# Where the weights' parts lie in SBUF against the tokens' parts, and three 256-column products per block in a gated short-convolution layer

## The chip, the cores and the metric

The kernel runs on one core of one Trainium2 chip. Times are device microseconds (us). The kernel before takes 954.23 us, the median of three runs (953.26 to 955.2). Engines: PE is TensorE (PEld its weight loads), DVE is VectorE, ACT is ScalarE, SP issues the DMAs.

## The reference, cut to what matters

One layer on 256 tokens of width 2048, with branches of width E = 4096, all in float32:

```python
h = rmsnorm(x, norm_g)                                  # (256, 2048)
shift, scale, gate = split(silu(c) @ ada_w + ada_b, 3)  # ada_w: 2048 x 6144
h = h * (1 + scale) + shift
b, cg, v, g = split(h @ w_in, 4)                        # w_in: 2048 x 16384
u = causal_depthwise_conv(cg * v, conv_w)               # three taps
y = b * u * silu(g)
x = x + gate * (y @ w_out)                              # w_out: 4096 x 2048
return rmsnorm(x, final_g)
```

## The kernel before, in words

**Split products.** Matmuls run in float32r. To keep float32's accuracy every operand is split into a rounded part and the rest: a weight tile `raw` becomes `hi` (ACT, L191) and `lo` (DVE, L192); the tokens become `hh` and `hl`, the first and second 256 columns of `hT[:, k, :]` (L261, L262); y becomes `yh` and `yl` (L206, L207). Each product of two matrices is then hi·hh + hi·hl + lo·hh, summed in PSUM. TensorE holds a 128x128 stationary operand and streams a moving operand past it. In the two input stages the weights' parts are stationary and the tokens' parts move; in the output stage y's parts are stationary and the weights' parts move.

**Stages.** (1) Up to about 60 us the tokens are normed and transposed, and the first sums of `ada_w` are made. (2) Up to about 410 us, the first 16 of 32 column tiles of each quarter of `w_in` (`part`, L264 to L300): four column tiles at a time, in pieces of `k` (the 16 blocks of the contraction) as `shift` and `scale` come ready, with an order that `plan()` sets. Each block (k, column tile) takes three matmuls of 256 columns: L286 hi·hh, L291 hi·hl, L292 lo·hh. Two column tiles share a PSUM bank. The sums go to `acc` (L298, L300); when a group of channels is whole, `mixed` makes y of it. DVE forms the sums of `ada_w` here as well (L238), and from about 300 us those of its gate third (`gate_piece`, L359). (3) Up to about 763 us, the two-tile stage: the other 16 column tiles, two at a time (L365 to L405), over the four quarters. Each block takes one matmul of 512 columns (L382, hi against hh and hl side by side, which fills a bank: hi·hh in its first half, hi·hl in its second) and one of 256 (L385, lo·hh into the first half). There are 8 pairs of tiles x 4 quarters x 2 tiles x 16 k = 1024 blocks. At the end of a quarter ACT copies the second half of each of the two banks to `z` (L391) and DVE adds the first (L392); the quarter's own operation follows from `z` (L396, L401, L402, L404). (4) The output stage: 4 column groups x 32 tiles x 2 token halves x 3 = 768 matmuls of 512 columns, L427 hi·yh, L428 lo·yh, L429 hi·yl. Then the gate, the second norm and the stores.

**Order and buffers.** Each engine runs its own stream in order; a scheduler with a cost model of its own sets it when the program is built. There are three buffers each for `raw`, `hi` and `lo`, all of 8192 bytes per partition, and six PSUM banks for sums.

**Places in SBUF.** Pools on the left grow upwards, pools on the right downwards from the top. In the built program `hi` and `lo` (left) start at 64 modulo 256 bytes, `hT` and the slots that hold y (right) at 224 modulo 256. All pieces inside these tiles step by multiples of 512 bytes, so that the remainders hold for every operand.

Of the kernel before, what the change touches and what calls it, by code (L numbers as in the profile page):

```python
# [8 lines left out]
F32 = mybir.dt.float32  # L9
F32R = mybir.dt.float32r  # L10
AF = mybir.ActivationFunctionType
ALU = mybir.AluOpType

P = 128
D = 2048
E = 4096
T = 256
KT = D // P
# [70 lines left out]
def short_conv_layer(ctx: ExitStack, tc: tile.TileContext, x, c, norm_g, ada_w, ada_b, w_in, conv_w, w_out, final_g, out):  # L89
    nc = tc.nc  # L90
    PSUM = bass.MemoryType.PSUM

    const = ctx.enter_context(tc.tile_pool(name="const", bufs=1))
    adap = ctx.enter_context(tc.tile_pool(name="adap", bufs=2))
    wpool = ctx.enter_context(tc.tile_pool(name="wpool", bufs=2))
    psum = ctx.enter_context(tc.tile_pool(name="psum", bufs=6, space=PSUM))
    hpool = ctx.enter_context(tc.tile_pool(name="hpool", bufs=1, side="right"))
    slots = ctx.enter_context(tc.tile_pool(name="slots", bufs=NSLOT, side="right"))

    def slot(shape, name, dtype=F32):  # L100
# [5 lines left out]
    after = mybir.DependencyInfo(mybir.DependencyClass.NoSync, mybir.DependencyReason.DATA)  # L106
# [59 lines left out]
    hT = hpool.tile([P, KT, 2 * T], F32R, tag="big", name="hT")  # L166
    hh_ = hT[:, :, 0:T]
# [40 lines left out]


    acc = {}  # L210
    gjunk = const.tile([P, P], F32, tag="gjunk", name="gjunk")
    adas = ada_w[0].rearrange("(k p) (s f) -> p k s f", p=P, s=3)

    sums = {}
# [1 line left out]
    def ada_piece(k0, nk, piece):  # L216
        w = nk * P
        kk = ASLOT // (2 * w)
        if piece == 0:
            sums[k0] = adap.tile([P, 2, 2 * P], F32, tag="gv", name="gv")  # L220
        gv = sums[k0]

        turns = [gv[:, :, i * w : (i + 1) * w] for i in range(2 if k0 == 0 and nk == 1 else 1)]
        j = piece * kk
        if k0 == 0:
            at = wpool.tile([P, SLOT], F32, tag=("lo", "hi")[piece % 2], name="at0", bufs=3)[:, :ASLOT]
        else:
            at = adap.tile([P, ASLOT], F32, tag="at", name="at", bufs=4)
        at4 = at.rearrange("p (k s f) -> p k s f", k=kk, s=2)
        for s in range(2):  # L230
            nc.sync.dma_start(at4[:, :, s, :], adas[:, j : j + kk, s, k0 * P : k0 * P + w])  # L231
        for i in range(kk):
            c_k = silu_c[:, j + i : j + i + 1]
            g2 = turns[(j + i) % len(turns)]
            if j + i < len(turns):
                nc.vector.tensor_scalar_mul(g2, at4[:, i], c_k)
            else:
                nc.vector.scalar_tensor_tensor(out=g2, in0=at4[:, i], scalar=c_k, in1=g2, op0=ALU.mult, op1=ALU.add)  # L238
        if j + kk < KT:
            return  # L240
        if len(turns) == 2:
            nc.vector.tensor_tensor(out=turns[0], in0=turns[0], in1=turns[1], op=ALU.add)

        tp = psum.tile([P, 4, P], F32, tag="sm", name="tp_g", bufs=2)
        gs = const.tile([P, 4], F32, tag="gs", name="gs", bufs=2)
        for o in range(2 * nk):
            nc.tensor.transpose(tp[:, o, :], gv[:, o // nk, (o % nk) * P : (o % nk + 1) * P], ident)
        for o in range(2 * nk):
            nc.scalar.activation(gjunk, tp[:, o, :], AF.Copy, accum_out=gs[:, o : o + 1])
        ks = slice(k0, k0 + nk)  # L250
        nc.vector.tensor_tensor(out=scale[:, ks], in0=gs[:, nk : 2 * nk], in1=b_scale[:, ks], op=ALU.add)
        nc.vector.tensor_tensor(out=shift[:, ks], in0=gs[:, 0:nk], in1=b_shift[:, ks], op=ALU.add)
        nc.vector.scalar_tensor_tensor(
            out=scale[:, ks], in0=scale[:, ks], scalar=1.0, in1=gT[:, ks], op0=ALU.add, op1=ALU.mult
        )
        for k in range(k0, k0 + nk):
            hf = xs[k // CT][:, k % CT, :]
            nc.vector.tensor_scalar(
                out=hf, in0=hf, scalar1=scale[:, k : k + 1], scalar2=shift[:, k : k + 1], op0=ALU.mult, op1=ALU.add
            )  # L260
            nc.scalar.copy(hh_[:, k], hf)  # L261
            nc.vector.tensor_tensor(out=hl_[:, k], in0=hf, in1=hh_[:, k].bitcast(F32), op=ALU.subtract)  # L262

    def part(ch, q, k0, k1):  # L264

        col = q * E + ch * CT * P
        step = SLOT // (CT * P)
        banks = [psum.tile([P, 512], F32, tag="mm", name="mm_s") for _ in range(CT // 2)]
        for s0 in range(k0, k1, step):
            sk = min(step, k1 - s0)  # L270
            n = sk * CT * P
            raw = raw_tile("raw_s")
            nc.sync.dma_start(
                raw[:, :n].rearrange("p (k f) -> p k f", k=sk),
                w_in[0, s0 * P : (s0 + sk) * P, col : col + CT * P].rearrange("(k p) f -> p k f", p=P),
            )
            hi, lo = split(raw, n)
            for i in range(sk):
                k = s0 + i
                hh, hl = hh_[:, k], hl_[:, k]  # L280
                for m in range(CT):
                    o = slice((i * CT + m) * P, (i * CT + m + 1) * P)
                    dst = banks[m // 2][:, (m % 2) * T : (m % 2 + 1) * T]

                    opens = k == k0 and m % 2 == 0
                    first = nc.tensor.matmul(dst, hi[:, o], hh, start=opens, stop=False, skip_group_check=True)  # L286
                    if opens:
                        opener = first
                    elif k == k0:
                        tc.add_manual_dep(first.ins, opener.ins.name, after, reason="the bank's flags are cleared first")  # L290
                    nc.tensor.matmul(dst, hi[:, o], hl, start=False, stop=False, skip_group_check=True)  # L291
                    nc.tensor.matmul(dst, lo[:, o], hh, start=False, stop=k == k1 - 1, skip_group_check=True)  # L292
        if k0 == 0:
            acc[ch, q] = slot([P, CT, T], f"acc{ch}{q}")
        for b, bank in enumerate(banks):
            a = acc[ch, q][:, 2 * b : 2 * b + 2, :].rearrange("p a t -> p (a t)")
            if k0 == 0:
                nc.scalar.copy(a, bank)  # L298
            else:
                nc.vector.tensor_tensor(out=a, in0=bank, in1=a, op=ALU.add)  # L300
# [65 lines left out]
    n_piece = 0  # L366
    for ct in range(NS, NCT, 2):
        for q in QUARTERS:
            banks = [psum.tile([P, 2, T], F32, tag="mm", name="mm_b") for _ in range(2)]
            col = q * E + ct * P  # L370
            for kp in range(0, KT, KP):
                raw = raw_tile("raw")
                nc.sync.dma_start(
                    raw.rearrange("p (k f) -> p k f", k=KP),
                    w_in[0, kp * P : (kp + KP) * P, col : col + 2 * P].rearrange("(k p) f -> p k f", p=P),
                )
                hi, lo = split(raw, SLOT)
                for m in range(2):
                    for i in range(KP):
                        k = kp + i  # L380
                        o = slice((i * 2 + m) * P, (i * 2 + m + 1) * P)
                        nc.tensor.matmul(  # L382
                            banks[m].rearrange("p a t -> p (a t)"), hi[:, o], hT[:, k, :], start=k == 0, stop=False, skip_group_check=True
                        )
                        nc.tensor.matmul(banks[m][:, 0, :], lo[:, o], hh_[:, k], start=False, stop=k == KT - 1, skip_group_check=True)  # L385
                n_piece += 1
                if n_piece % 2 == 0:
                    gate_piece()
            z = zs[q // 2][:, q % 2]
            for m in range(2):  # L390
                nc.scalar.copy(z[:, m, :], banks[m][:, 1, :])  # L391
                nc.vector.tensor_tensor(out=z[:, m, :], in0=banks[m][:, 0, :], in1=z[:, m, :], op=ALU.add)  # L392
            if q == 1:
                zc = z
            elif q == 2:
                nc.vector.tensor_tensor(out=zc, in0=z, in1=zc, op=ALU.mult)  # L396
                for j in range(2):
                    conv(ct + j, z[:, j, :], zc[:, j, :])
                u = z
            elif q == 3:  # L400
                nc.scalar.activation(z, z, AF.Silu)  # L401
                nc.vector.tensor_tensor(out=u, in0=u, in1=z, op=ALU.mult)  # L402
            else:
                nc.vector.tensor_tensor(out=u, in0=z, in1=u, op=ALU.mult)  # L404
                split_y(ys[ct // 2], u)  # L405
    while gate_todo:
        gate_piece()
# [118 lines left out]
```

## Time and profile before

| | |
|---|---|
| median of three runs | 954.23 us |
| the profiled execution's own time | 952.04 us |
| its span | 950.2 us |
| mean granted clock of TensorE | 0.99 |
| PE, PEld, DVE, ACT busy in the span | 918.3, 835.4, 681.4, 419.3 us |
| DMA | 227.51 MB, mean 239 GB/s |

How to read it: a matmul's duration counts from its start until its result is written, and the next one starts while it still runs, so that durations of neighbours overlap and their sum is above the span. What a matmul costs on the path is the distance between one start and the next. A weight load runs beside the matmul before the one that it is for.

### The profile page before, as it was taken

Reading aid. Unit: us, or ns where it says so; the run is one execution under the profiler, and the core shown is the slowest. Engines: PE = TensorE matmul, PEld = TensorE weight load, DVE = VectorE, ACT = ScalarE, POOL = GpSimd, SP = SyncE. Lnnn points to the kernel's source line nnn. Section 1 sums busy time; section 2 is a strip of 40 time slices with the busy share of each in tenths; the row PEclk is TensorE's granted clock in tenths of the full one; section 3 lists DMA queues with packets and bytes.
Section 4 is the critical chain, followed back from the end, with each engine's and each line's share of the span. In section 5 each row is a group of like instructions: output and inputs, shape, how many; then the busy total and the mean of one; then the engine's idle time right before and its main releaser. Section 6 shows DMA issues by size and latency. Waiting matters only on the chain.

```text
span 950.2 us, 14332 instructions
## 1 busy us (share of the span) xinstructions
PE 918.3 (97%) x5963; PEld 835.4 (88%) x5963; DVE 681.4 (72%) x789; ACT 419.3 (44%) x470; POOL 0.7 (0%) x6
## 2 busy tenths in 40 slices
PE   2799999999999999999999999999999999999996
PEld 2699999999999999988888888888888878888885
DVE  4799998999999998997465556555555654544882
ACT  6575343443435544444443444444444433343333
POOL 0000000000000000000000000000000000000000
PEclk9799999999999999999999999999999999999998
DMA  9999997999989787886665565566555685555542
GB/s 273 299 360 368 291 335 253 323 347 319 350 278 308 243 271 240 281 288 208 193 201 181 185 199 193 178 193 201 181 178 190 206 313 177 180 199 196 178 133 88
DMA packets 172048, 227.51 MB, mean 239 GB/s; under 512 B 5792, under 2 KB 112464, under 8 KB 171600
## 3 DMA queue, kind: packets, MB, share of 16 engines
q1 hardware_dynamic: 171984, 226.61, 72.9%
q8 instruction: 46, 0.75, 0.3%
q14 instruction: 18, 0.15, 0.0%
HBM read 224.49 MB, written 2.10 MB: 238 GB/s over the span
## 4 chain that ended last, share of the span: by engine, by line
PE 91%; DMA 4%; DVE 2%; issue 1%; SPq 1%; ACT 0%; ACTq 0%; DVEq 0%
PE mm_b L382 25%; PE mm_b L385 13%; PE mm_s L292 11%; PE mm_s L286 11%; PE mm_s L291 11%; PE mm_o L428 6%; PE mm_o L427 6%; PE mm_o L429 6%; DMA at<-in_ada_w_dram 2%; DMA raw_s<-in_sc_w_in_dram 2%; DVE lo L192 1%; DMA x<-in_x_dram 1%; DVE gv L238 1%; SPq L231 0%; PE ps_gate L362 0%
## 5 line engine op out<-in xcount | busy, mean ns | idle before, releaser
L382 PE MATMUL mm_b<-hT,hi 128*128 128x512 f32 x1024 | 355.2, 392 | 0.0
L286 PE MATMUL mm_s<-hT,hi 128*128 128x256 f32 x1024 | 286.9, 284 | 7.5 <-ACT hT L261 4.9
L291 PE MATMUL mm_s<-hT,hi 128*128 128x256 f32 x1024 | 287.7, 283 | 0.0
L385 PE MATMUL mm_b<-hT,lo 128*128 128x256 f32 x1024 | 285.4, 280 | 0.0
L292 PE MATMUL mm_s<-hT,lo 128*128 128x256 f32 x1024 | 283.6, 283 | 1.7 <-DVE lo L192 1.7
L192 DVE TENSOR_TENSOR lo<-raw,hi 128x2048 fp32r<-128x2048 f32 x64 | 146.6, 2291 | 128.4 <-ACT hi L191 128.4
L382 PEld LDWEIGHTS mm_b<-hT,hi 128*128 128x128 f32 x1024 | 192.0, 188 | 42.3 <-issue 0.2
L191 ACT CAST hi<-raw_s 128x2048 fp32r<-128x2048 f32 (+3 forms) x85 | 126.5, 1488 | 177.1 <-PE mm_s L291 128.6
L286 PEld LDWEIGHTS mm_s<-hT,hi 128*128 128x128 f32 x1024 | 194.4, 191 | 8.5 <-ACT hT L261 5.1
L291 PEld LDWEIGHTS mm_s<-hT,hi 128*128 128x128 f32 x1024 | 195.5, 191 | 0.2 <-issue 0.2
L292 PEld LDWEIGHTS mm_s<-hT,lo 128*128 128x128 f32 x1024 | 192.6, 191 | 2.6 <-DVE lo L192 2.4
L385 PEld LDWEIGHTS mm_b<-hT,lo 128*128 128x128 f32 x1024 | 192.3, 188 | 0.5 <-issue 0.2
L191 ACT CAST hi<-raw 128x2048 fp32r<-128x2048 f32 x64 | 122.4, 1912 | 158.0 <-PE mm_b L382 103.1
L192 DVE TENSOR_TENSOR lo<-raw_s,hi 128x2048 fp32r<-128x2048 f32 (+3 forms) x85 | 149.5, 1759 | 19.9 <-ACT hi L191 19.5
L192 DVE TENSOR_TENSOR lo<-raw_o,hi 128x2048 fp32r<-128x2048 f32 x32 | 73.3, 2290 | 67.0 <-ACT hi L191 67.0
L191 ACT CAST hi<-raw_o 128x2048 fp32r<-128x2048 f32 x32 | 61.2, 1913 | 103.8 <-PE mm_o L429 93.6
L428 PE MATMUL mm_o<-lo,y 128*128 128x512 f32 x256 | 101.7, 399 | 0.0
L427 PE MATMUL mm_o<-hi,y 128*128 128x512 f32 x256 | 101.0, 396 | 0.0
L429 PE MATMUL mm_o<-hi,y 128*128 128x512 f32 x256 | 100.1, 392 | 0.0
L238 DVE SCALAR_TENSOR_TENSOR gv<-at,silu_c,gv 128x512 f32<-128x512 f32 (+1 forms) x149 | 92.2, 639 | 3.8 <-DMA at<-in_ada_w_dram 3.0
L427 PEld LDWEIGHTS mm_o<-hi,y 128*128 128x128 f32 x256 | 48.1, 188 | 12.6 <-issue 0.2
L429 PEld LDWEIGHTS mm_o<-hi,y 128*128 128x128 f32 x256 | 48.1, 188 | 11.6
(84 smaller groups left out, 457.8 us busy)
## 6 DMA issues: line engine op xcount, KB each, us to landing
raw<-in_sc_w_in_dram SPq DMA_DIRECT2D x64, 1024.0 KB, 5.6
raw_s<-in_sc_w_in_dram SPq DMA_DIRECT2D x46, 1024.0 KB, 7.3
at<-in_ada_w_dram SPq DMA_DIRECT2D x128, 256.0 KB, 6.7
raw_o<-in_sc_w_out_dram SPq DMA_DIRECT2D x32, 1024.0 KB, 5.1
at_g<-in_ada_w_dram SPq DMA_DIRECT2D x32, 512.0 KB, 6.9
raw_s<-in_sc_w_in_dram SPq DMA_DIRECT2D x19, 512.0 KB, 5.4
raw_s<-in_sc_w_in_dram SPq DMA_DIRECT2D x7, 768.0 KB, 7.7
raw_s<-in_sc_w_in_dram SPq DMA_DIRECT2D x13, 256.0 KB, 4.4
```

Source lines behind the costliest of these rows:

```text
L191: nc.scalar.copy(hi[:, :n], raw[:, :n])
L192: nc.vector.tensor_tensor(out=lo[:, :n], in0=raw[:, :n], in1=hi[:, :n].bitcast(F32), op=ALU.subtract)
L238: nc.vector.scalar_tensor_tensor(out=g2, in0=at4[:, i], scalar=c_k, in1=g2, op0=ALU.mult, op1=ALU.add)
L286: first = nc.tensor.matmul(dst, hi[:, o], hh, start=opens, stop=False, skip_group_check=True)
L291: nc.tensor.matmul(dst, hi[:, o], hl, start=False, stop=False, skip_group_check=True)
L292: nc.tensor.matmul(dst, lo[:, o], hh, start=False, stop=k == k1 - 1, skip_group_check=True)
L382: nc.tensor.matmul(banks[m].rearrange("p a t -> p (a t)"), hi[:, o], hT[:, k, :], start=k == 0, stop=False, skip_group_check=True)
L385: nc.tensor.matmul(banks[m][:, 0, :], lo[:, o], hh_[:, k], start=False, stop=k == KT - 1, skip_group_check=True)
L427: nc.tensor.matmul(po, yh, hi[:, o], start=opens, stop=False, skip_group_check=True)
L428: nc.tensor.matmul(po, yh, lo[:, o], start=False, stop=False, skip_group_check=True)
L429: nc.tensor.matmul(po, yl, hi[:, o], start=False, stop=ct == NCT - 1, skip_group_check=True)
```

## The change

Two small pools of padding are put on the right: 56 floats (224 bytes) above `hT`, and 48 floats (192 bytes) between `hT` and the slots. With these, `hT` starts at 0 modulo 256 and the slots at 64; `hi` and `lo` stay at 64. So in stages 2 and 3 the stationary parts lie 64 bytes past the moving ones (modulo 256; before: 96 past), and in the output stage both lie at the same remainder (before: the stationary ones 160 past). `gjunk`, 512 bytes that took an unused result, is left out, and that result is written over its source in PSUM.

In the two-tile stage a block takes the same three products of 256 columns as in stage 2, through a function that both now call, and the two tiles of a quarter share one bank. At a quarter's end one operation reads the bank where before four made `z` and one more used it.

```diff
+    line = ctx.enter_context(tc.tile_pool(name="line", bufs=1, side="right"))
+    line.tile([P, 56], F32, tag="line", name="line")
...
     hpool = ctx.enter_context(tc.tile_pool(name="hpool", bufs=1, side="right"))
+    line2 = ctx.enter_context(tc.tile_pool(name="line2", bufs=1, side="right"))
+    line2.tile([P, 48], F32, tag="line2", name="line2")
...
-    gjunk = const.tile([P, P], F32, tag="gjunk", name="gjunk")
...
-            nc.scalar.activation(gjunk, tp[:, o, :], AF.Copy, accum_out=gs[:, o : o + 1])
+            nc.scalar.activation(tp[:, o, :], tp[:, o, :], AF.Copy, accum_out=gs[:, o : o + 1])
...
+    def products(dst, hi, lo, k, begins, ends, left):
+        opens = begins and left
+        first = nc.tensor.matmul(dst, hi, hh_[:, k], start=opens, stop=False, skip_group_check=True)
...
+        nc.tensor.matmul(dst, hi, hl_[:, k], start=False, stop=False, skip_group_check=True)
+        nc.tensor.matmul(dst, lo, hh_[:, k], start=False, stop=ends, skip_group_check=True)
...
-            banks = [psum.tile([P, 2, T], F32, tag="mm", name="mm_b") for _ in range(2)]
+            bank = psum.tile([P, 2, T], F32, tag="mm", name="mm_b")
...
-                        nc.tensor.matmul(
-                            banks[m].rearrange("p a t -> p (a t)"), hi[:, o], hT[:, k, :], start=k == 0, stop=False, skip_group_check=True
-                        )
-                        nc.tensor.matmul(banks[m][:, 0, :], lo[:, o], hh_[:, k], start=False, stop=k == KT - 1, skip_group_check=True)
+                        products(bank[:, m, :], hi[:, o], lo[:, o], k, k == 0, k == KT - 1, m == 0)
...
-            for m in range(2):
-                nc.scalar.copy(z[:, m, :], banks[m][:, 1, :])
-                nc.vector.tensor_tensor(out=z[:, m, :], in0=banks[m][:, 0, :], in1=z[:, m, :], op=ALU.add)
             if q == 1:
+                nc.scalar.copy(z, bank)
                 zc = z
             elif q == 2:
-                nc.vector.tensor_tensor(out=zc, in0=z, in1=zc, op=ALU.mult)
+                nc.vector.tensor_tensor(out=zc, in0=bank, in1=zc, op=ALU.mult)
...
             elif q == 3:
-                nc.scalar.activation(z, z, AF.Silu)
+                nc.scalar.activation(z, bank, AF.Silu)
...
             else:
-                nc.vector.tensor_tensor(out=u, in0=z, in1=u, op=ALU.mult)
+                nc.vector.tensor_tensor(out=u, in0=bank, in1=u, op=ALU.mult)
```

Up to the end of stage 2 the streams of PE, DVE, ACT and SP stand in the order that they had before. TensorE's stream at the place where the two-tile stage ends and the output stage begins (`ps_gate` is the last sum for the gate, `mm_b` the bank or banks of a quarter, `mm_o` one of the output's banks); before:

```order
L382 MATMUL mm_b<-hT,hi 128x512
L385 MATMUL mm_b<-hT,lo 128x256
L362 MATMUL ps_gate<-gacc,ones 128x512
L427 MATMUL mm_o<-hi,y_3552 128x512
L428 MATMUL mm_o<-lo,y_3552 128x512
L429 MATMUL mm_o<-hi,y_3552 128x512
```

After:

```order
L274 MATMUL mm_b<-hT,hi 128x256
L279 MATMUL mm_b<-hT,hi 128x256
L280 MATMUL mm_b<-hT,lo 128x256
L371 MATMUL ps_gate<-gacc,ones 128x512
L431 MATMUL mm_o<-hi,y_3559 128x512
L432 MATMUL mm_o<-lo,y_3559 128x512
L433 MATMUL mm_o<-hi,y_3559 128x512
```

Nothing has moved past another thing; each block of the two-tile stage has one matmul more and the same columns.

DVE's stream in the middle of the two-tile stage, from the end of a block of the second quarter on (`z_4640` and `z_4641` hold the quarters' values, L192 makes the weights' `lo`); before:

```order
L392 TENSOR_TENSOR z_4641<-mm_b,z_4641 128x256
L192 TENSOR_TENSOR lo<-raw,hi 128x2048
L392 TENSOR_TENSOR z_4641<-mm_b,z_4641 128x256
L396 TENSOR_TENSOR z_4640<-z_4641,z_4640 128x512
L192 TENSOR_TENSOR lo<-raw,hi 128x2048
L198 SCALAR_TENSOR_TENSOR z_4641<-z_4640,cw,z_4641 128x255 x2
L392 TENSOR_TENSOR z_4641<-mm_b,z_4641 128x256
L201 SCALAR_TENSOR_TENSOR z_4641<-z_4640,cw,z_4641 128x254 x2
```

After:

```order
L400 TENSOR_TENSOR z_4647<-mm_b,z_4647 128x512
L197 TENSOR_TENSOR lo<-raw,hi 128x2048
L203 SCALAR_TENSOR_TENSOR z_4648<-z_4647,cw,z_4648 128x255 x2
L206 SCALAR_TENSOR_TENSOR z_4648<-z_4647,cw,z_4648 128x254 x2
L197 TENSOR_TENSOR lo<-raw,hi 128x2048 x2
L406 TENSOR_TENSOR z_4648<-z_4648 128x512
```

The three additions in these rows (L392) are gone, and the product of two quarters, L396 before and L400 after, reads the bank itself.

More of the change, by code (lines that the diff above doesn't have):

```diff
@@ L262, in ada_piece @@
             nc.vector.tensor_tensor(out=hl_[:, k], in0=hf, in1=hh_[:, k].bitcast(F32), op=ALU.subtract)
+    opener = [None]
+    def products(dst, hi, lo, k, begins, ends, left):
+        opens = begins and left
+        first = nc.tensor.matmul(dst, hi, hh_[:, k], start=opens, stop=False, skip_group_check=True)
+        if opens:
+            opener[0] = first
+        elif begins:
+            tc.add_manual_dep(first.ins, opener[0].ins.name, after, reason="the bank's flags are cleared first")
+        nc.tensor.matmul(dst, hi, hl_[:, k], start=False, stop=False, skip_group_check=True)
+        nc.tensor.matmul(dst, lo, hh_[:, k], start=False, stop=ends, skip_group_check=True)
     def part(ch, q, k0, k1):
@@ L279, in part @@
                 k = s0 + i
-                hh, hl = hh_[:, k], hl_[:, k]
                 for m in range(CT):
@@ L283, in part @@
                     dst = banks[m // 2][:, (m % 2) * T : (m % 2 + 1) * T]
[L285 to L292, printed above, removed]
+                    products(dst, hi[:, o], lo[:, o], k, k == k0, k == k1 - 1, m % 2 == 0)
         if k0 == 0:
```

## The prediction

> **What bounds the kernel now.** First the page: who is busy, and what the chain that ended last is made of.
>
> ```profile
> span 950.2 us, 14332 instructions
> PE 918.3 (97%) x5963; PEld 835.4 (88%) x5963; DVE 681.4 (72%) x789; ACT 419.3 (44%) x470; POOL 0.7 (0%) x6
> PEclk9799999999999999999999999999999999999998
> PE 91%; DMA 4%; DVE 2%; issue 1%; SPq 1%; ACT 0%; ACTq 0%; DVEq 0%
> PE mm_b L382 25%; PE mm_b L385 13%; PE mm_s L292 11%; PE mm_s L286 11%; PE mm_s L291 11%; PE mm_o L428 6%; PE mm_o L427 6%; PE mm_o L429 6%; DMA at<-in_ada_w_dram 2%; DMA raw_s<-in_sc_w_in_dram 2%; DVE lo L192 1%; DMA x<-in_x_dram 1%; DVE gv L238 1%; SPq L231 0%; PE ps_gate L362 0%
> ```
>
> TensorE holds 91% of the chain, at full clock after the start. Then the windows of the three stages, with one tight stretch of the first (columns: length, PE, PEld, DVE, ACT, POOL busy with instruction counts, clock, DMA share, GB/s):
>
> ```profile
> 60.00:410.00 350.00, 349.52 (x2929) 347.99 (x2928) 323.15 (x411) 155.27 (x184) 0.00 (x0) 1.00 0.92 303
> 300.00:340.00 40.00, 40.00 (x329) 39.04 (x328) 40.00 (x56) 21.42 (x23) 0.00 (x0) 1.00 0.81 254
> 412.00:762.00 350.00, 350.00 (x2019) 307.78 (x2018) 211.25 (x209) 156.68 (x159) 0.00 (x0) 1.00 0.61 195
> 764.00:942.00 178.00, 178.00 (x764) 143.21 (x763) 101.14 (x67) 65.74 (x52) 0.00 (x0) 1.00 0.53 182
> ```
>
> TensorE never stops in any of them. In the first, DVE stands close behind: 323 of 350 us, and 40 of 40 in one stretch. In the other two it has room (60% and 57%). So the time is the number of matmuls by the distance from start to start, and the distances come next, from the timeline's first and last rows of a stretch each: 13 steps of the 256-column matmuls, 10 blocks of the two-tile stage, 12 steps of the output stage.
>
> ```profile
> 249.83 0.28 PE L292 MATMUL mm_s<-hT,lo 128*128 128x256 f32 x1
> 251.39 0.28 PE L286 MATMUL mm_s<-hT,hi 128*128 128x256 f32 x1
> ...
> 499.71 0.39 PE L382 MATMUL mm_b<-hT,hi 128*128 128x512 f32 x1
> 503.17 0.39 PE L382 MATMUL mm_b<-hT,hi 128*128 128x512 f32 x1
> ...
> 799.69 0.39 PE L429 MATMUL mm_o<-hi,y 128*128 128x512 f32 x1
> 802.49 0.39 PE L429 MATMUL mm_o<-hi,y 128*128 128x512 f32 x1
> ```
>
> That is 1.56/13 = 120 ns, 3.46/10 = 346 ns a block, and 2.80/12 = 233 ns. Over its whole stretch the first stage has 349.52/2929 = 119.3 ns. Are these distances what streaming must take? The groups of four windows speak against it (137 to 155 us, 70 to 90, 175.79 to 175.85 with one matmul in it, and 770 to 920; behind the first bar stand the busy us and the mean ns of one):
>
> ```profile
> L286 PE MATMUL mm_s<-hT,hi 128*128 128x256 f32 x51 | 14.3, 283 | 0.0
> ...
> L286 PE MATMUL mm_s<-hT,hi 128*128 128x256 f32 x57 | 15.4, 280 | 0.0
> ...
> L291 PE MATMUL mm_s<-hT,hi 128*128 128x256 f32 x1 | 0.3, 277 | 0.0
> ...
> L428 PE MATMUL mm_o<-lo,y 128*128 128x512 f32 x215 | 85.8, 399 | 0.0
> L427 PE MATMUL mm_o<-hi,y 128*128 128x512 f32 x215 | 84.7, 394 | 0.0
> L429 PE MATMUL mm_o<-hi,y 128*128 128x512 f32 x214 | 83.9, 392 | 0.0
> ```
>
> The same line with the same operands takes 283 ns in one stretch and 280 in another; nothing in the code differs there. The third row is the matmul at 175.58, behind which no weight load could run, since the next one waited for `lo`:
>
> ```profile
> 176.33 0.19 PEld L292 LDWEIGHTS mm_s<-hT,lo 128*128 128x128 f32 x1 [0.68 <-DVE lo L192]
> ```
>
> Alone it took 277 ns. In the output stage two matmuls of one shape differ by 7 ns, by which parts of y and the weights they read. So a matmul is slowed by something that depends on the load beside it and on the phase of the two streams. That is what places in memory could change.
>
> **The change part by part.** *The places, stage 2.* What would a 256-column matmul cost undisturbed? Three rows give bounds. Four transposes, each with a load of its own, step at 0.44/4 = 110 ns:
>
> ```profile
> 90.77 0.44 PE tp_g L247 x4
> ```
>
> Next, a block's two matmuls in the two-tile stage:
>
> ```profile
> L382 PE MATMUL mm_b<-hT,hi 128*128 128x512 f32 x964 | 334.8, 392 | 0.0
> L385 PE MATMUL mm_b<-hT,lo 128*128 128x256 f32 x966 | 269.5, 280 | 0.0
> ```
>
> 256 columns more cost 392 - 280 = 112 ns. And the lone matmul, 6 ns shorter than those that step at 120, gives 114. Above stands no change at all, 119.3, or the worst row, 120. I take 111, between the first two: they need no second assumption, where the lone matmul is one case and may still carry what a bad start place costs by itself. For TensorE alone the stage would shrink to 350 x 111/119.3 = 326 us, 24 less. But DVE has 323 us of work in it, in the same order as before, and waits now and then; I let the stage end at 332, with DVE at 97%: **-18 us**. Ends: -30 (109 ns, DVE hidden after all) and +2 (120 ns).
>
> *Three products, two-tile stage.* 1024 blocks each lose 346 ns and gain three matmuls. At 111 ns: 1024 x (346 - 333) = **-13 us**. Ends: at 109, -19; at 120, +14. The point of balance is 346/3 = 115.3 ns. The streamed columns are the same 768, so the edit pays only what a third start and a third load cost, and it rests wholly on the places. DVE's 211 of 350 us leave room for the shorter stage.
>
> *The places, output stage.* Here the 512-column matmul would cost 111 + 112 = 223 ns where it now costs 233: 768 x 10 = **-8 us**. Ends: twice 109 gives -12; all like the slowest row, L428, 4 ns above the mean of the three lines (399 against 395), gives +3.
>
> *The quarter's end.* Of these groups the first two go, and the third reads the bank:
>
> ```profile
> L392 DVE TENSOR_TENSOR z<-mm_b,z 128x256 f32<-128x256 f32 x64 | 26.6, 416 | 0.0
> L391 ACT COPY z<-mm_b 128x256 f32<-128x256 f32 x64 | 23.5, 368 | 20.0 <-PE mm_b L385 20.0
> L401 ACT ACTIVATE z<-z 128x512 f32<-128x512 f32 x8 | 5.1, 632 | 17.0 <-DVE z L392 17.0
> ```
>
> That is 26.6 us of DVE and 23.5 of ACT, less eight copies of 128x512 (about 0.6 us each by L401's row). It lies beside a TensorE whose only wait from 60 to 942 us is this one, so I cost it at nothing:
>
> ```profile
> PE mm_s L292 <- DVE lo L192: 0.5, 1, 0.5
> ```
>
> Were the cover gone, the edit would help, not harm. One wait is new in kind: L400, L405 and L408 wait for a whole quarter's bank, and behind them on DVE and ACT stand the next weights' `lo` and `hi`. Each wait was there before, on the same last matmul (L391's 20.0 us), and the row above says that `lo` is never late in this stage. A quarter now holds one bank of six instead of two, so TensorE gets banks no later.
>
> *The unused result into PSUM.* This group writes elsewhere:
>
> ```profile
> L249 ACT ACTIVATE gjunk<-tp_g 128x128 f32<-128x128 f32 x32 | 8.9, 279 | 8.8 <-PE tp_g L247 8.2
> ```
>
> The 32 instructions take 0.28 us each, and only the first few, ahead of 60 us, have no matmuls beside them: nothing, within 1 us either way.
>
> Sum: -18 - 13 - 8 = -39. The profiled execution took 952.0 us (1.8 of it outside the span), 2.2 below the median of the runs; against the median, 954.2 - 39 = **915 us**.
>
> **A rule that speaks against it.** The rows show a matmul of 277 ns alone and 280 to 283 beside a load. The Trainium skill, "TensorE: Matmul & The Clock Gate", Part 2, says that TensorE reads SBUF through two independent ports and that loading the next weights "doesn't steal SBUF read bandwidth from the running matmul". By that rule places change nothing; this is the first rival below. As far as the one lone matmul bears it out, the trace disagrees, by 3 to 6 ns. The same page, "Back-to-back issue gap", gives N/2.4 + 2.5 ns: 109 ns for 256 columns, 216 for 512. By it, as an estimate, the three terms would be -18 (DVE still the limit), -19 and -13, so 904; the trace before stands 10 to 17 ns above these gaps.
>
> **The rivals.**
>
> *Places mean nothing (chance 0.15).* Then the first and third terms are 0, and in the two-tile stage each block pays for its third start: 1024 x (3 x 119.3 - 346) = +12 us, **966 us**. For it: the difference of 280 to 283 in one line at unchanged places shows that phase alone does something. Against it: the 7 ns between L428 and L429, same shapes, other places. It decides wherever the new distance stays above 115.3 ns without a gain elsewhere.
>
> *The new places are worse (0.05).* A load and a stream that begin at the same remainder, or 64 bytes apart, could meet more often than at 96 and 160. If every 256-column matmul stepped at 122 and every 512-column one like L428: +8 + 20 + 3, **985 us**. Against it: no row now shows a 256-column matmul above the 120 of the tightest stretch.
>
> *A part only (0.20).* The lone matmul's 114 ns is the floor, since what is left has another cause: 350 x 114/119.3 = 334, so -16; 1024 x (346 - 342) = -4; output 768 x (233 - 226) = -5: **929 us**.
>
> *DVE takes over (0.10).* In the stretch from 300 to 340 us DVE is full already and TensorE lives on buffers. If DVE's waits don't shrink with the stage, it gives 5 us at most: -5 - 13 - 8, **928 us**. The slack that TensorE gains would then show as waits for `lo`.
>
> **How the numbers follow.** The forecast has 0.50. About 0.2%, 2 us, is what a measurement of this kernel can tell from no change. Slower are the first two rivals, 0.20. No change, 0.04, comes out of the part-only case where terms cancel. Faster: the rest, 0.76. The range begins at the sum of the low ends (-30 - 19 - 12, 893), and reaches through the part-only case to 956, the upper edge of no change; left out is the slower 0.20. The forecast's own range is 893 to 930.
>
> **What would show it right or wrong.** Right: 256-column matmuls in both input stages stepping at 109 to 113 ns, with one duration per line in every stretch; output matmuls at 216 to 225 with L431, L432 and L433 alike; the two-tile stage near 341 us; DVE above 95% from 60 us to the stage's end and some waits of TensorE for L197. Wrong: distances of 117 to 120 as before, with 358 ns a block; the three output lines still 7 ns apart; or TensorE waiting in the two-tile stage for a bank, for `hi` or for `lo`.

## The result, and the profile after

The changed kernel takes 927.03 us (median of 4 runs, 926.73 to 930.5) against 953.75 before (4 runs, 951.4 to 955.2): a ratio of 0.973, with a 95% interval of 0.970 to 0.976. It is 27 us faster; 39 were forecast. The profiled execution is the slowest of the four (930.5 us, span 928.7), so that the traces show 21.5 us of difference in the span, and the rest is not in them.

The page after: who is busy, and the chain that ended last.

```profile
span 928.7 us, 16264 instructions
PE 895.0 (96%) x6987; PEld 859.1 (93%) x6987; DVE 658.3 (71%) x725; ACT 401.6 (43%) x414; POOL 0.7 (0%) x6
PE 87%; DMA 5%; DVE 4%; issue 1%; ACT 1%; SPq 1%; ACTq 0%; DVEq 0%
```

TensorE still carries the chain, with 1024 matmuls more than before. Its groups in the three stages that matter (`mm_s` is stage 2, `mm_b` the two-tile stage, `mm_o` the output; busy us, then mean ns of one):

```profile
L279 PE MATMUL mm_s<-hT,hi 128*128 128x256 f32 x1024 | 283.7, 279 | 0.0
L274 PE MATMUL mm_b<-hT,hi 128*128 128x256 f32 x1024 | 283.0, 276 | 0.0
L279 PE MATMUL mm_b<-hT,hi 128*128 128x256 f32 x1024 | 282.6, 276 | 0.0
L280 PE MATMUL mm_b<-hT,lo 128*128 128x256 f32 x1024 | 282.6, 276 | 0.0
L431 PE MATMUL mm_o<-hi,y 128*128 128x512 f32 x256 | 99.7, 391 | 0.0
L432 PE MATMUL mm_o<-lo,y 128*128 128x512 f32 x256 | 99.3, 389 | 0.0
L433 PE MATMUL mm_o<-hi,y 128*128 128x512 f32 x256 | 99.3, 389 | 0.0
```

In the two-tile stage the 256-column matmul lasts 276 ns where it lasted 280, in stage 2 279 where it lasted 283. The three lines of the output stage, which lay 7 ns apart, are alike (L431's mean holds the stage's first matmul, which took 0.80 us behind the sum for the gate). The distance from start to start, first and last row of 32 steps in the two-tile stage and of 15 in the output stage, from the timeline:

```profile
599.82 0.28 PE L274 MATMUL mm_b<-hT,hi 128*128 128x256 f32 x1
603.45 0.28 PE L280 MATMUL mm_b<-hT,lo 128*128 128x256 f32 x1
...
799.71 0.39 PE L432 MATMUL mm_o<-lo,y 128*128 128x512 f32 x1
803.11 0.39 PE L432 MATMUL mm_o<-lo,y 128*128 128x512 f32 x1
```

That is 3.63/32 = 113.4 ns for 256 columns (340 a block, against 346), and 3.40/15 = 226.7 for 512 (against 233). The one is twice the other.

Stage 2 does not step at 113 throughout. Two of its stretches (200 to 220 us and 235 to 255 us):

```profile
L274 PE MATMUL mm_s<-hT,hi 128*128 128x256 f32 x60 | 16.6, 276 | 0.0
...
L274 PE MATMUL mm_s<-hT,hi 128*128 128x256 f32 x58 | 16.3, 281 | 0.0
```

At the same places and in the same line it takes 276 ns for a while and 281 for another. In the trace it steps at 118 up to 67 us, from 90 to 127 and from 227 to 262, changing each time at the transposes of a new `k`, and mostly at 113 elsewhere; the mean of the stage's steps from 60 us on, leaving out those above 150 ns, is 114.5 (before: 118.6). The windows of the stages (columns as before), and TensorE's one wait in the first of them:

```profile
60.00:397.00 337.00, 335.42 (x2913) 333.85 (x2913) 318.74 (x405) 153.36 (x183) 0.00 (x0) 1.00 0.93 311
398.00:746.00 348.00, 348.00 (x3067) 347.52 (x3066) 194.34 (x154) 140.97 (x105) 0.00 (x0) 1.00 0.63 201
748.00:921.00 173.00, 173.00 (x765) 143.21 (x763) 99.45 (x64) 64.66 (x51) 0.00 (x0) 1.00 0.56 188
```

```profile
PE mm_s L280 <- DVE lo L197: 1.5, 2, 1.0
```

From the first matmul of a stage to the first of the next: the two-tile stage begins at 397.2 us (before 406.8) and the output stage at 746.7 (763.1); the last matmul starts at 921.0 (942.5). So stage 2 gave 9.6 us, the two-tile stage 6.8, the output stage 5.1.

### The profile page after: what moved, and what is told of

It is laid out like the page before. It is cut to its first block, busy times and chain, and to the rows that moved or that the text cites. A ratio compares the mean times of both kernels' runs of the same rounds, so it can differ in the third digit from the quotient of the medians.

```text
span 928.7 us, 16264 instructions
## 1 busy us (share of the span) xinstructions
PE 895.0 (96%) x6987; PEld 859.1 (93%) x6987; DVE 658.3 (71%) x725; ACT 401.6 (43%) x414; POOL 0.7 (0%) x6
## 4 chain that ended last, share of the span: by engine, by line
PE 87%; DMA 5%; DVE 4%; issue 1%; ACT 1%; SPq 1%; ACTq 0%; DVEq 0%
PE mm_b L274 13%; PE mm_b L279 13%; PE mm_b L280 12%; PE mm_s L280 10%; PE mm_s L274 10%; PE mm_s L279 10%; PE mm_o L431 6%; PE mm_o L433 6%; PE mm_o L432 6%; DMA raw_s<-in_sc_w_in_dram 3%; DMA at<-in_ada_w_dram 2%; DVE lo L197 2%; DVE gv L242 1%; DMA x<-in_x_dram 1%; ACT hi L196 1%
## 5 line engine op out<-in xcount | busy, mean ns | idle before, releaser
L274 PE MATMUL mm_s<-hT,hi 128*128 128x256 f32 x1024 | 283.5, 281 | 9.1 <-ACT hT L265 4.8
L279 PE MATMUL mm_s<-hT,hi 128*128 128x256 f32 x1024 | 283.7, 279 | 0.0
L274 PE MATMUL mm_b<-hT,hi 128*128 128x256 f32 x1024 | 283.0, 276 | 0.0
L279 PE MATMUL mm_b<-hT,hi 128*128 128x256 f32 x1024 | 282.6, 276 | 0.0
L280 PE MATMUL mm_b<-hT,lo 128*128 128x256 f32 x1024 | 282.6, 276 | 0.0
L280 PE MATMUL mm_s<-hT,lo 128*128 128x256 f32 x1024 | 279.8, 280 | 2.2 <-DVE lo L197 2.2
L197 DVE TENSOR_TENSOR lo<-raw,hi 128x2048 fp32r<-128x2048 f32 x64 | 146.7, 2292 | 128.9 <-ACT hi L196 128.8
L280 PEld LDWEIGHTS mm_s<-hT,lo 128*128 128x128 f32 x1024 | 191.3, 190 | 3.5 <-DVE lo L197 3.5
L279 PEld LDWEIGHTS mm_b<-hT,hi 128*128 128x128 f32 x1024 | 192.2, 188 | 0.2 <-issue 0.2
L274 PEld LDWEIGHTS mm_b<-hT,hi 128*128 128x128 f32 x1024 | 192.2, 188 | 0.2 <-issue 0.2
L280 PEld LDWEIGHTS mm_b<-hT,lo 128*128 128x128 f32 x1024 | 192.2, 188 | 0.0
L197 DVE TENSOR_TENSOR lo<-raw_s,hi 128x2048 fp32r<-128x2048 f32 (+3 forms) x85 | 149.4, 1757 | 15.7 <-ACT hi L196 15.2
L197 DVE TENSOR_TENSOR lo<-raw_o,hi 128x2048 fp32r<-128x2048 f32 x32 | 73.3, 2291 | 67.8 <-ACT hi L196 67.8
L431 PE MATMUL mm_o<-hi,y 128*128 128x512 f32 x256 | 99.7, 391 | 0.0
L433 PE MATMUL mm_o<-hi,y 128*128 128x512 f32 x256 | 99.3, 389 | 0.0
L432 PE MATMUL mm_o<-lo,y 128*128 128x512 f32 x256 | 99.3, 389 | 0.0
```

Source lines behind the costliest of these rows:

```text
L197: nc.vector.tensor_tensor(out=lo[:, :n], in0=raw[:, :n], in1=hi[:, :n].bitcast(F32), op=ALU.subtract)
L274: first = nc.tensor.matmul(dst, hi, hh_[:, k], start=opens, stop=False, skip_group_check=True)
L279: nc.tensor.matmul(dst, hi, hl_[:, k], start=False, stop=False, skip_group_check=True)
L280: nc.tensor.matmul(dst, lo, hh_[:, k], start=False, stop=ends, skip_group_check=True)
L431: nc.tensor.matmul(po, yh, hi[:, o], start=opens, stop=False, skip_group_check=True)
L432: nc.tensor.matmul(po, yh, lo[:, o], start=False, stop=False, skip_group_check=True)
```

## The experiments

**The theories.** *Distance*: what counts is how far, modulo 256 bytes, the stationary operand starts from the moving one. *Own start*, the rival: what counts is where each tile itself starts, modulo 64; the change also moved `hT` from 224 to 0 and y from 224 to 64. *Products*: a part of the gain belongs to the three short products, whatever the places.

**One half of the change each.** First the places alone: the two paddings in, `gjunk` out, the two-tile stage as before.

```diff
+    line.tile([P, 56], F32, tag="line", name="line")
...
+    line2.tile([P, 48], F32, tag="line2", name="line2")
...
-    gjunk = const.tile([P, P], F32, tag="gjunk", name="gjunk")
```

> The kernel before with the two paddings and without gjunk; the two-tile stage keeps its 512-column and 256-column product and its four operations per quarter. If the places carry the whole gain, a block costs 226.7 + 113.3 = 340 ns, which is also three times 113.3, and the kernel takes 927 us within 2. If the three products carry a part of it (the long product steps worse than two short ones, say 229 as before), a block costs 343 to 346 ns and the kernel takes 930 to 934.

Measured: 942.44 us against 951.96, a ratio of 0.9902 (0.9878 to 0.9926). Neither number was met. Stage 2 and the output stage step as in the changed kernel; the two-tile stage is worse than before. Its groups, and the first and last start of ten blocks:

```profile
L385 PE MATMUL mm_b<-hT,hi 128*128 128x512 f32 x1024 | 361.9, 398 | 0.0
L388 PE MATMUL mm_b<-hT,lo 128*128 128x256 f32 x1024 | 286.9, 281 | 0.0
```

```profile
499.83 0.40 PE L385 MATMUL mm_b<-hT,hi 128*128 128x512 f32 x1
503.37 0.40 PE L385 MATMUL mm_b<-hT,hi 128*128 128x512 f32 x1
```

A block costs 354 ns, where it cost 346 at the old places and 340 with three products. The long product lasts 398 ns (392 before), and the short one 281, although it has the operands and the distance of stage 2's matmuls, which last 276 wherever that stage steps at 113.

Then the products alone: the changed kernel without its paddings.

```diff
-    line.tile([P, 56], F32, tag="line", name="line")
...
-    line2.tile([P, 48], F32, tag="line2", name="line2")
```

> The changed kernel without the two paddings, so that hT and y start at 224 modulo 256 again and the weights' parts at 64. If the places carry the gain, stage 2 and the output stage step as before (118.6 and 233 ns) and a block of the two-tile stage costs 3 x 118.6 = 356 ns against 346: 954 + 10 = 964 us. If places mean nothing, about 927.

Measured: 961.5 us against 951.96, a ratio of 1.0088 (1.0059 to 1.0116). A matmul of the two-tile stage and the slowest line of the output stage:

```profile
L270 PE MATMUL mm_b<-hT,hi 128*128 128x256 f32 x1024 | 287.7, 281 | 0.0
L428 PE MATMUL mm_o<-lo,y 128*128 128x512 f32 x256 | 101.7, 399 | 0.0
```

The three products step at 118.3 ns here, 355 a block: the third product costs what it was expected to, and the three products alone gain nothing. The ratios of the two halves, 0.9902 and 1.0088, multiply to 0.999; together the halves give 0.973. They need each other.

**Distance or own start.** Two kernels with other paddings (in floats; `line` above `hT`, `line3` on the left ahead of the weights' parts, `line2` above y). All three tiles moved by 32 bytes, distances as changed:

```diff
-    line.tile([P, 56], F32, tag="line", name="line")
+    line.tile([P, 48], F32, tag="line", name="line")
...
+    line3.tile([P, 8], F32, tag="line3", name="line3")
```

> The changed kernel with all three tiles 32 bytes further (hT at 32, weights' parts at 96, y at 96 modulo 256): the distances between stationary and moving operand stay 64 and 0. Theory of the distance (only stationary start minus moving start modulo 256 counts): 113.3 and 226.7 ns and 927 us as the changed kernel. Theory of the own start (a tile that does not start at a multiple of 64 costs a further step by itself): 116 to 119 ns in the input stages, 229 to 235 in the output stage, 940 us or more.

And the distances of before at other places:

```diff
+    line3.tile([P, 8], F32, tag="line3", name="line3")
...
-    line2.tile([P, 48], F32, tag="line2", name="line2")
```

> hT at 0, weights' parts at 96, y at 0 modulo 256: the distances of the kernel before (96 in the input stages, 160 in the output stage) at other places of their own; three products per block. Theory of the distance: 118.6 ns in the input stages and 231 to 238 ns in the output stage, as the kernel before with three products, 964 us. Theory of the own start: only the weights' parts start off a multiple of 64, so the input stages' moving operand is undisturbed and they gain (113 to 116 ns), 930 to 945 us.

Measured: 931.35 us (ratio 0.9776, 0.9752 to 0.9800) and 960.11 us (1.0079, 1.0058 to 1.0100). Of the first:

```profile
L276 PE MATMUL mm_b<-hT,hi 128*128 128x256 f32 x1024 | 283.0, 276 | 0.0
L434 PE MATMUL mm_o<-lo,y 128*128 128x512 f32 x256 | 99.3, 389 | 0.0
```

Of the second:

```profile
L274 PE MATMUL mm_b<-hT,hi 128*128 128x256 f32 x1024 | 287.7, 281 | 0.0
L431 PE MATMUL mm_o<-hi,y 128*128 128x512 f32 x256 | 101.0, 396 | 0.0
L432 PE MATMUL mm_o<-lo,y 128*128 128x512 f32 x256 | 101.7, 399 | 0.0
L433 PE MATMUL mm_o<-hi,y 128*128 128x512 f32 x256 | 100.1, 392 | 0.0
```

With every tile off a multiple of 64 the durations are those of the changed kernel; with `hT` and y at 0 and the old distances they are those of the kernel before, down to the 7 ns between two lines of the output stage (392, 396, 399). The theory of the own start has fallen. In the traces the first is 2.9 us longer than the changed kernel, all of it in stage 2: TensorE stood 1.9 us there at 169 us, and its clock fell for some 20 matmuls (window 171 to 174 us, granted clock 0.59 behind the busy times):

```profile
171.00:174.00 3.00, 2.83 (x14) 2.83 (x15) 3.00 (x8) 0.47 (x2) 0.00 (x0) 0.59 0.61 176
```

**Which distances.** Seven more kernels, all with `line` at 56 floats; `line3` and `line2` set the rest:

| distance in the input stages, output stage | line3 | line2 |
|---|---|---|
| 0, 128 | 48 | 32 |
| 128, 64 | 16 | 16 |
| 192, 32 | 32 | 8 |
| 64, 192 | none | none |
| 32, 224 | 56 | none |
| 160, 96 | 24 | none |
| 224, 64 | 40 | 56 |

> The changed kernel with other paddings: hT at 0, weights' parts at 0, y at 128 modulo 256, so distance 0 in the input stages and 128 in the output stage. If any distance that is a multiple of 64 is good, 113.3 and 226.7 ns in both and 927 us. If only 64 (for 256 columns) and 0 (for 512) are good, 116 to 122 and 231 to 238 ns, 945 to 970 us.

> hT at 0, weights' parts at 128, y at 192 modulo 256: distance 128 in the input stages, 64 in the output stage. If any multiple of 64 is good, 113.3 and 226.7 ns, 927 us. If each length has its own good distance, the output stage shows what 64 does to 512 columns beside nothing but 512 columns: 235 ns as the long product in the run with the places alone, or 226.7 if that 235 comes from the change of lengths.

> hT at 0, weights' parts at 192, y at 224 modulo 256: distance 192 in the input stages, 32 in the output stage. If any multiple of 64 is good, 113.3 ns in the input stages; 32 is no multiple, so the output stage steps at 231 to 238 as at 160. About 932 us. If only single distances are good, 116 to 122 ns, 950 to 970 us.

> The changed kernel without its second padding: hT at 0, weights' parts at 64, y at 0 modulo 256, distance 64 in the input stages as changed, 192 in the output stage. If any multiple of 64 is good, 226.7 ns and 927 us: the second padding is worth nothing. If not, 231 to 238 ns in the output stage and 931 to 936 us.

> The changed kernel with hT at 0, weights' parts at 32, y at 0 modulo 256: distance 32 in the input stages, 224 in the output stage. If the good place is a single one, 117 to 120 ns and 229 to 235 ns, 955 to 965 us. If it is a span that reaches 32 bytes to either side, 113.4 in the input stages or 226.7 in the output stage (192 gave 229, so a slope towards 0 would give 227 to 229).

> hT at 0, weights' parts at 160, y at 0 modulo 256: distance 160 in the input stages, 96 in the output stage. Both lie far from the good places: 117 to 120 ns and 231 to 235 ns, 957 to 965 us.

> hT at 0, weights' parts at 224, y at 32 modulo 256: distance 224 in the input stages, 64 in the output stage. Input stages 117 to 120 ns. The output stage has the distance that gave 233.3 ns with y at 192 and the weights' parts at 128; if the distance alone counts, 233.3 again. 957 to 965 us.

Measured, in this order: 965.34, 961.39, 957.68, 931.89, 960.84, 970.31 and 951.48 us, against 951.55 (first four) and 951.98 (last three); each of them but the last differs from its kernel before by more than its interval. The last two lie outside the 957 to 965 us that were expected, one above and one below. The mean distance from start to start, worked out from all starts of a stage but one (each stage has a single step above 500 ns, behind a sum for the gate), by the distance of the operands (96 and 160 are the run with the old distances, 64 and 0 the changed kernel):

| distance, bytes modulo 256 | 0 | 32 | 64 | 96 | 128 | 160 | 192 | 224 |
|---|---|---|---|---|---|---|---|---|
| 256 columns, two-tile stage, ns | 120.0 | 118.3 | **113.4** | 118.3 | 118.7 | 120.0 | 117.8 | 116.7 |
| 512 columns, output stage, ns | **226.7** | 233.3 | 233.3 | 234.3 | 232.4 | 233.3 | 228.9 | 233.3 |

(At distance 64 the output stage was run at two pairs of places: 233.3 both times.) So neither any multiple of 64 nor a span is good: among the eight distances tried each length has one that is best, 64 for 256 columns and 0 for 512, and all others cost 3 to 7 ns and 2 to 8 ns. The rows of the run with 0 and 128, and of the one with 64 and 192:

```profile
L281 PE MATMUL mm_b<-hT,hi 128*128 128x256 f32 x1024 | 290.1, 283 | 0.0
```

```profile
L277 PE MATMUL mm_b<-hT,hi 128*128 128x256 f32 x1024 | 283.0, 276 | 0.0
L429 PE MATMUL mm_o<-hi,y 128*128 128x512 f32 x256 | 99.6, 390 | 0.0
L431 PE MATMUL mm_o<-hi,y 128*128 128x512 f32 x256 | 100.6, 394 | 0.0
```

Distance 0, the best for the output stage, is one of the two worst for the input stages. The second padding is worth the 2 ns of 768 matmuls, 1.7 us.

The table has one or a few runs for each distance, and a stage can change its step at unchanged places. Distance 192 shows it: in stage 2 of that run the step is 113.3 ns from 66 to 90 us, as at distance 64, and 117.8 afterwards. One line from 68 to 88 us and from 200 to 220:

```profile
L276 PE MATMUL mm_s<-hT,hi 128*128 128x256 f32 x60 | 16.0, 276 | 0.0
...
L276 PE MATMUL mm_s<-hT,hi 128*128 128x256 f32 x58 | 16.2, 279 | 0.0
```

So the short step is not distance 64's alone. What the runs show is that at 64 it held throughout the two-tile stage in all three kernels with three products, and at no other distance did a two-tile stage reach it. How the other distances rank among themselves is not shown.

**Why the places alone spoil the long product.** The two-tile stage's long product at distance 64 is the case of the table's 233.3. The run with the places alone was done again with its products in another order: per piece of weights first the 16 long ones, then the 16 short ones.

```diff
                 for m in range(2):
                     for i in range(KP):
...
                         nc.tensor.matmul(
                             banks[m].rearrange("p a t -> p (a t)"), hi[:, o], hT[:, k, :], start=k == 0, stop=False, skip_group_check=True
                         )
+                for m in range(2):
+                    for i in range(KP):
...
                         nc.tensor.matmul(banks[m][:, 0, :], lo[:, o], hh_[:, k], start=False, stop=k == KT - 1, skip_group_check=True)
```

> The run with the places alone (two paddings, long and short product per block), but in the two-tile stage the 16 long products of a piece of weights come first and the 16 short ones after. If length and distance decide, each by itself, the long ones step at 233 ns as the output stage did at distance 64, the short ones at 113.4: a block costs 347 ns against 353 alternating, and the kernel takes 935 us. If only the change from one length to the other did the harm, 226.7 + 113.3 = 340 ns and 928 us. If the long product spoils what follows whatever the order, 353 ns and 942 us.

Measured: 937.48 us (ratio 0.9843, 0.9826 to 0.9859).

```profile
L385 PE MATMUL mm_b<-hT,hi 128*128 128x512 f32 x1024 | 249.4, 396 | 0.0
L392 PE MATMUL mm_b<-hT,lo 128*128 128x256 f32 x1024 | 126.8, 276 | 0.0
```

The long ones step at 233.0 ns, the short ones at 113.7, 347 a block as expected: in runs of one length, length and distance decide, and in this order the short product gets its 276 ns back. Alternating costs 6.6 ns a block more (353.3 against 346.7). So at distance 64 neither of the two orders reaches the 340 of three short ones, and with the shared places of `hi` and `lo` and one `hT` for both input stages the short products fit this distance best.

Alternating is not always the worse order. In the kernel before, at distance 96, the long product steps at 229.2 ns and the short one at 117.5, 347 a block, where the table's 234.3 and 118.3 would make 353. What mixed lengths cost can't be added up from the table; why is open.

## Why the prediction was right, and where it put the gain too high

*TensorE's distance is the time*: right. The three stages gave 9.6 + 6.8 + 5.1 = 21.5 us, all of the span's difference.

*What is disturbed is a matmul beside a weight load, and places can change it*: that places change it is right, and shown by the table. That the load does it is argued: the distance between both operands counts, and the stationary one is read by the load; but a load runs beside every matmul that steps at 113.4 ns too, and no run took the load away. The rule weighed against it, of the Trainium skill's "TensorE: Matmul & The Clock Gate", Part 2, is that loading the next weights "doesn't steal SBUF read bandwidth from the running matmul". By that rule the distance should not matter; here the same instructions step at 113.4 ns at one distance and at up to 120.0 at others.

*The undisturbed price, 111 ns for 256 columns and 223 for 512*: this is the step that failed, in size. It is 113.4 and 226.7. I had set the lone matmul aside as one case that "may still carry what a bad start place costs by itself"; its 277 ns gave 114, and the groups after show 276. Neither of the two rows I leaned on prices this matmul. 392 - 280 = 112 was the difference of two disturbed matmuls; at the good distances it is 226.7 - 113.4 = 113.3. The 110 came from transposes that stream 128 columns, not 256. That 111 lay within 2.4 ns owes something to luck. The rival "A part only" was built on the lone matmul and gave 929 us; its floor of 114 is nearest the measured step, and what it took for a remainder with another cause is the smallest step that any distance gave. "DVE takes over" came as near in total, 928, with terms that did not hold: 5 us for stage 2, then 13 and 8.

*Stage 2, -18*: it gave 9.6. 2857 steps by 118.6 - 113.4 are 14.9 us; the stretches at 118 took back 2857 x (114.5 - 113.4) = 3.1. The steps above 150 ns, left out so far, hold 6.4 us after and 4.3 before, 2.1 more, all of it in stalls between 163 and 176 us: 14.9 - 3.1 - 2.1 = 9.7. The chain after shows what stands behind these stalls: a load of weights (DMA), its `hi` and `lo`, then the `hi` and `lo` of a later piece, for which L280 waits.

```profile
154.66 9.04 DMA raw_s<-in_sc_w_in_dram
...
163.80 1.92 ACT hi L196
...
165.74 1.54 DVE lo L197
...
171.40 1.93 ACT hi L196
173.35 2.30 DVE lo L197
...
175.70 0.39 PE mm_s L280
```

The waits are for `lo`, as the rival "DVE takes over" said, but they come to 1.5 us, where it let 13 go, and the chain behind them begins with a load that took 9 us. DVE is at 95% (318.74 of 337) without ending the stage; the cap at 332 us was not what held.

*Three products, -13*: 6.8. 1024 x (346 - 340) = 6.1 is the same sum with the right price. That the edit rests wholly on the places was right, and the run with the products alone, 9.5 us slower, 8.5 of them in this stage, bears out the sign of the first rival's two-tile term (+12). That the places in turn rest on the edit was not foreseen: left with its long product, the stage would have lost 6.7 us (355.8 to 362.5 from its first matmul to its last).

*The output stage, -8*: 5.1; 768 x 6.6.

*The quarter's end at nothing*: right. DVE's share of the two-tile stage fell from 211 to 194 us, ACT's from 157 to 141, in stretches of one length within 2 us, and TensorE waits for nothing there. The unused result, also put at nothing, is in both halves of the change, and no run took it alone.

Of the signs named ahead, these came: the three output lines alike, no wait in the two-tile stage, a few waits for L197. These did not: one duration per line in every stretch (276 and 281 in stage 2), 109 to 113 ns (113.4), 216 to 225 (226.7), a two-tile stage near 341 us (349.5).

The other rivals: places that are worse than before exist (distances 0 and 160 step at 120.0 ns in the input stages), but they are not these. Why the good distance is 64 for the one length and 0 for the other is open; no run took the load's own timing apart.

## What to carry to other kernels

Where TensorE is busy all the time, measure the distance from start to start, and compare a matmul's duration with that of one behind which no load ran: what is above it may be the next weights' load meeting the stream. In this kernel the start of the stationary operand against the moving one, modulo 256 bytes, decided 3 to 6% of a 256-column matmul and 1 to 3% of a 512-column one. To set it costs only padding, and the best one differed between the two lengths. Mixing lengths at one distance can lose what the distance gives, so places and shapes have to be tried together. Look at the step in several stretches: it can change at unchanged places.

## What the runs showed of the hardware

- In float32r a matmul's smallest mean distance was 113.4 ns for 256 columns and 226.7 for 512: twice the columns, twice the time, so that these two lengths show no fixed part. The Trainium skill's "TensorE: Matmul & The Clock Gate", "Back-to-back issue gap", gives N/2.4 + 2.5 ns for an isolated matmul, which as an estimate would be 109 and 216.
- The distance of the operands counts modulo 256, not 128 and not 512. For 128: the output stage steps at 226.7 ns at distance 0 and at 232.4 at 128, the two-tile stage at 113.4 at 64 and at 117.8 at 192. For 512: by its paddings the run with the old distances has its operands 256 bytes further apart or nearer, modulo 512, than the run with the products alone, and the durations are the same, 281 and 392 to 399 ns.
- The stream can fall into another step at unchanged places: 113 or 118 ns in stage 2 of the changed kernel, for up to 37 us at a time, changing at transposes and stalls, and the same two steps at distance 192.
